# Three places where half-height float32 products of two heads are put side by side in TensorE's queue

## The chip, the cores and the metric

One core of one Trainium2 chip. The metric is the device time of one execution in microseconds (us). The kernel before was run three times: 2778.02, 2770.26 and 2773.04 us, median 2773.04 us.

## The reference, cut to what matters

Two layers, 512 tokens, 1024 channels. Each layer is a feed-forward half step, a mixing step and a second feed-forward half step. The mixing step projects the normed input once and runs three branches on it; the change lies in two of them.

```python
# RWKV-7 branch, 8 heads of 64 channels
w_log = -softplus(-(w0 + tanh(xw) @ decay_b)) - 0.5      # decay: a product over 64 channels
a     = sigmoid(a0 + xa @ iclr_b)                        # in-context rate: a product over 64 channels
...
for t: state = state*w_t - (state @ kk_t) b_t + v_t k_t ; y_t = state @ r_t

# band attention, 8 heads of 64 channels, QK-norm, 512 tokens in chunks of 64
scores = einsum('bnqhd,bnkhd->bnhqk', q, k) * 64**-0.5   # a product over 64 channels
probs  = softmax(scores + bias) ;  out = probs @ v

x = x + W_out(sum_b sigmoid(gate_b) * (y_b @ W_branch_b))
```

The delta-rule scan over time is computed in 8 chunks of 64 steps. A chunk needs the state at its start, a triangular system for the corrections of the chunk, the state at its end, and y of the chunk, which is a sum of two products.

## The kernel before, in words

Heads are worked on two at a time: a tile of 128 partitions holds head u = 0 on partitions 0 to 63 and head u = 1 on 64 to 127 (`H2`; `W2` names the same two halves the other way round). There are four such pairs (`p`) in a layer.

**Big and small products.** The weight products (projections, gates, branch and output matrices, feed-forward) run in float16 with the weight and the input split in a high and a low part, three matmuls for each 128 rows (`mm3`). The RWKV and attention inner products run in float32. A float32 matmul appears in the trace as two instructions, so a row of N products counts 2N.

**The order.** Nothing is issued where it is written. Each call is recorded (`Recorder`, `Plan.note`), and `Plan.run` then simulates the five engines with the costs in `Plan.cost`, always takes the ready operation with the longest tail behind it, and writes out one fixed order for each engine. On TensorE a float16 sum may be put ahead of a small operation when small ones have had more than their share (`RATIO`, `DEBT`). What stands inside one `plan.block()` is one operation for the planner: its matmuls stay together in TensorE's queue, in the order written. Where its simulation sees TensorE idle for more than 0.4 us it puts in filling matmuls (`plan.warm`, on tile `wt`). All instructions are issued from line 538, so profile rows are told apart by tiles and shapes.

**PSUM.** Float16 sums use the buffers `g` (two); `a_ps()` gives one of two buffers for the attention branches (tile `as`), `s_ps()` one of two for RWKV (tile `s`); a ring hands them out in the order of the program, and a buffer waits for the last reader of what it held before. The scan has a bank of its own for y (`yp`) and one for its other products (`xps`).

**The band attention** (`band`). For a pair of heads there are four blocks `b` of 128 queries. `soft(b, u)` takes one buffer, computes the scores of one head (contraction over that head's 64 partitions, 128 queries by `nk = 128 (b + 1)` keys), adds the bias, and does the softmax; `turn` transposes the result in another buffer and copies it out. The units go in the order (b, 0), (b, 1), each `turn` one unit behind its `soft`.

**The RWKV branch** (`rwkv`). For each pair, first the decay: a product over partitions 0 to 63 of `xwa` into a buffer `s`, tanh on ScalarE, plus one on VectorE; then the in-context rate: a product over partitions 64 to 127 into the next buffer `s`, tanh. In the scan each chunk `c` has four blocks on TensorE: x (tiles `ar`, `gx` into `xps`), the corrections (`cx`, `tt`), the state step (`kk`/`kb0` and `ta`/`be`) and y. In y, head u gets first a product over all 128 partitions (`gx` with `vz`), then one over the 64 partitions of the other half (`g1` with `vu`) which adds to it:

```python
for u, h in enumerate(H2):
    o, w = yp[h, c * CH:(c + 1) * CH], W2[u]
    PE.matmul(o, lhsT=gx[:, c, u, CH:2 * CH], rhs=vz[:, c, u, :], start=True, stop=False)
    PE.matmul(o, lhsT=g1[w, c, :], rhs=vu[u][w, c, :], start=False, stop=True)
```

In the profile `vz` is tile `ar`, `g1` is `g`, and `vu` are `kk` and `ta`. The state for chunk c + 1 is written to `ar` by VectorE from `xps` and is what x of the next chunk waits for.

Of the kernel before, what the change touches and what calls it, by code (L numbers as in the profile page):

```python
# [10 lines left out]
AF = mybir.ActivationFunctionType  # L11
# [5 lines left out]
P = 128  # L17
# [8 lines left out]
CH = 64  # L26
# [529 lines left out]
def trunk(tc: tile.TileContext, i: dict, out: bass.AP, dbg: dict | None = None, depth: int = DEPTH):  # L556
    nc = tc.nc
    dbg = dbg or {}
    plan = Plan(tc)
    ctx = ExitStack()  # L560
    V, S, G, PE, D = plan.V, plan.S, plan.G, plan.PE, plan.D
# [42 lines left out]
    def s_ps():  # L604
        return pq.tile([P, T], F32, tag="s", name=nm("s"))

    def a_ps():
        return pa.tile([P, T], F32, tag="a", name=nm("as"))
# [291 lines left out]
    H2 = [slice(0, CH), slice(CH, P)]  # L900
    W2 = [slice(CH, P), slice(0, CH)]
# [69 lines left out]
    def mixing(l, pieces, kst):  # L971
        pv = pvs[l]
        lv = lvs[l]
# [104 lines left out]
        def band():  # L1078
            for p in range(NP):
                q_, k_, vt = att_of[p]  # L1080
                bias = ta_("bias", [P, 2, 2 * P])
                D.dma_start(out=bias, in_=i["bias"][l, p])
                V.memset(bias[0:CH, :, 2 * P - CH:2 * P], -1e30)
                sqs = []
                for t in (k_, q_):
                    sq = ta_("sc", bufs=3)
                    S.activation(sq, t, AF.Square)
                    sqs.append(sq)
                rs = []
                for sq in sqs:  # L1090
                    v = small("n8", 8)
                    V.tensor_scalar(out=v, in0=head_ss(sq, a_ps), scalar1=1.0 / CH, scalar2=1e-6, op0=ALU.mult, op1=ALU.add)
                    rs.append(rpow(v, 8))
                rq = small("rq", 8)
                V.tensor_scalar(out=rq, in0=rs[1], scalar1=CH ** -0.5, scalar2=None, op0=ALU.mult)
                V.scalar_tensor_tensor(out=k_, in0=k_, scalar=lv["aqk"], in1=head_bc(rs[0], a_ps), op0=ALU.mult, op1=ALU.mult)
                pt = []
                for u in range(2):
                    t = ta_("pt", [P, 1280], bufs=2)
                    pt.append([t[:, c0:c0 + T - b * P] for b, c0 in enumerate((0, 512, 896, 1152))])  # L1100

                def soft(b, u):
                    nk = (b + 1) * P
                    h = H2[u]
                    ps = a_ps()
                    PE.matmul(ps[:, :nk], lhsT=q_[h, b * P:(b + 1) * P], rhs=k_[h, 0:nk], start=True, stop=True)
                    sc = ta_("sc", bufs=3)
                    far = max(0, nk - 2 * P)
                    for c0, c1, bb in ((0, far, bias[:, u, 0:1].to_broadcast([P, far])), (far, nk, bias[:, u, 2 * P - (nk - far):2 * P])):
                        if c1 > c0:  # L1110
                            V.scalar_tensor_tensor(out=sc[:, c0:c1], in0=ps[:, c0:c1], scalar=rq[:, 2 * b + u:2 * b + u + 1], in1=bb, op0=ALU.mult, op1=ALU.add)
                    nx = small("nx")
                    V.tensor_reduce(out=nx, in_=sc[:, :nk], op=ALU.max, axis=AX.X, negate=True)
                    den = small("den")
                    S.activation(sc[:, :nk], sc[:, :nk], AF.Exp, bias=nx[:, 0:1], accum_out=den)
                    rd = small("rd")
                    V.reciprocal(rd, den)
                    V.tensor_scalar(out=sc[:, :nk], in0=sc[:, :nk], scalar1=rd[:, 0:1], scalar2=None, op0=ALU.mult)
                    return b, u, sc

                def turn(b, u, sc):
                    ps = a_ps()
                    with plan.block():
                        for kb in range(b + 1):
                            PE.transpose(ps[:, kb * P:(kb + 1) * P], sc[:, kb * P:(kb + 1) * P], ident)
                    for kb in range(b + 1):
                        S.activation(pt[u][kb][:, (b - kb) * P:(b - kb + 1) * P], ps[:, kb * P:(kb + 1) * P], AF.Copy)

                pend = []
                for b in range(4):  # L1130
                    for u in range(2):
                        pend.append(soft(b, u))
                        if len(pend) > 1:
                            turn(*pend.pop(0))
                turn(*pend.pop(0))
                ps = a_ps()
                with plan.block():
                    for kb in range(4):
                        for u in range(2):
                            PE.matmul(ps[H2[u], kb * P:T], lhsT=vt[:, kb, u * CH:(u + 1) * CH], rhs=pt[u][kb], start=(kb == 0), stop=(kb == 3))  # L1140
                y = tm("ya", bufs=5)
                S.activation(y, ps, AF.Copy)
                ya.append(y)
            m2 = small("vx")
            V.tensor_reduce(out=m2, in_=vm, op=ALU.max, axis=AX.X)
            s, d = scale_of_max(all_max(m2), pool=mp, tag="satt")
            for p in range(NP):
                y = tm("ya", [P, 2, T], F16, bufs=5)
                put(y, ya[p], s)
                ya[p] = y  # L1150
            ya.append(d)
# [83 lines left out]
        def rwkv():  # L1235
            for p in range(NP):
# [14 lines left out]
                else:  # L1251
                    D.dma_start(out=vfs[p], in_=v_)

                ps = s_ps()
                PE.matmul(ps, lhsT=glob["lw"][0:CH, cs], rhs=glob["xwa"][0:CH, :], start=True, stop=True)
                tz = tr("w", bufs=3)
                S.activation(tz, ps, AF.Tanh, scale=0.5, bias=lv["w0"][:, p:p + 1])
                V.tensor_scalar(out=tz, in0=tz, scalar1=1.0, scalar2=None, op0=ALU.add)
                ps = s_ps()
                PE.matmul(ps, lhsT=glob["lw"][CH:P, cs], rhs=glob["xwa"][CH:P, :], start=True, stop=True)  # L1260
                ta = tr("ta")
                S.activation(ta, ps, AF.Tanh, scale=0.5, bias=lv["a0"][:, p:p + 1])
                cu = tr("w", bufs=3)
                V.tensor_tensor_scan(out=cu, data0=con[:, C_CM:C_CM + T], data1=tz, initial=0.0, op0=ALU.mult, op1=ALU.add)

# [69 lines left out]
                ps = s_ps()  # L1335
# [41 lines left out]
                for c in range(NCH):  # L1377
                    xp_ = xps[:, 0:3 * CH]
                    with plan.block():
                        for u, w in enumerate(W2):  # L1380
                            PE.matmul(xp_[w, 0:CH], lhsT=gx[:, c, u, 0:CH], rhs=vz[:, c, u, :], start=True, stop=True)
                    x_ = tr("cx", [P, CH], bufs=2)
                    V.tensor_copy(x_, xp_[:, 0:CH])
                    with plan.block():
                        for w in W2:
                            PE.matmul(xp_[w, CH:2 * CH], lhsT=tt[w, c, :], rhs=x_[w, :], start=True, stop=True)
                    S.activation(vu[0][W2[0], c, :], xp_[W2[0], CH:2 * CH], AF.Copy, scale=-1.0)
                    V.tensor_scalar(out=vu[1][W2[1], c, :], in0=xp_[W2[1], CH:2 * CH], scalar1=-1.0, scalar2=None, op0=ALU.mult)
                    if c < NCH - 1:
                        with plan.block():  # L1390
                            for u, w in enumerate(W2):
                                PE.matmul(xp_[w, 2 * CH:3 * CH], lhsT=kb[u][:, c, :], rhs=vu[u][:, c, :], start=True, stop=True)
                        if c:
                            zc = tr("czc", [P, 2, CH], bufs=2)
                            V.tensor_scalar(out=zc, in0=vz[:, c, :, :], scalar1=aw[:, c:c + 1], scalar2=None, op0=ALU.mult)
                        for u, w in enumerate(W2):
                            z = vz[w, c + 1, u, :]
                            if c:
                                V.scalar_tensor_tensor(out=z, in0=xp_[w, 2 * CH:3 * CH], scalar=aw[w, c:c + 1], in1=zc[w, u, :], op0=ALU.mult, op1=ALU.add)
                            elif u:  # L1400
                                V.tensor_scalar(out=z, in0=xp_[w, 2 * CH:3 * CH], scalar1=aw[w, c:c + 1], scalar2=None, op0=ALU.mult)
                            else:
                                S.activation(z, xp_[w, 2 * CH:3 * CH], AF.Copy, scale=aw[w, c:c + 1])
                    with plan.block():
                        for u, h in enumerate(H2):
                            o, w = yp[h, c * CH:(c + 1) * CH], W2[u]
                            PE.matmul(o, lhsT=gx[:, c, u, CH:2 * CH], rhs=vz[:, c, u, :], start=True, stop=False)
                            PE.matmul(o, lhsT=g1[w, c, :], rhs=vu[u][w, c, :], start=False, stop=True)


# [267 lines left out]
```

## Time and profile before

| | |
|---|---|
| median of three runs | 2773.04 us (2770.26 to 2778.02) |
| the profiled execution, its own time | 2773.73 us |
| its span in the trace | 2771.9 us |
| granted TensorE clock, mean | 0.999 |
| TensorE matmuls busy | 2745.1 us, 99% |
| VectorE busy | 1626.2 us, 59% |
| ScalarE busy | 1538.0 us, 55% |
| DMA, mean | 90 GB/s |

The layers' mixing steps with RWKV and attention lie at about 420 to 930 us and 1800 to 2310 us of the span. A matmul's row gives its start as recorded and an end that is modelled, and matmuls overlap; what a piece of work costs TensorE is read from start to start, and not from the durations.

### The profile page before, as it was taken

To read this page: it belongs to the slowest core of one execution; us is meant where nothing else is said; L and a number is where in the kernel's file an instruction comes from. 1 tells how busy PE (TensorE), PEld (TensorE's weight loads), DVE (VectorE), ACT (ScalarE), POOL (GpSimd) and SP (SyncE) were. 2 spreads that over 40 slices of the span, in tenths; PEclk is the share of its full clock that TensorE was granted. 3 is DMA by queue.
4 is the path that set the end of the run, shared out by engine and by line. 5 is a ranking of instruction groups with operands and counts; after the bars stand their busy time and mean duration, and the time that the engine had idled before them with its cause. 6 is when DMAs were issued, how large, how long until landed. Compare 5 with 4: busy or idle time off the path is not lost. (4 is left out here: it accounts for less than half of the span.)

```text
span 2771.9 us, 45458 instructions
## 1 busy us (share of the span) xinstructions
PE 2745.1 (99%) x18153; PEld 1496.6 (54%) x18153; DVE 1626.2 (59%) x4391; ACT 1538.0 (55%) x2543; POOL 111.1 (4%) x285
## 2 busy tenths in 40 slices
PE   9999999999999999999999999999999999999999
PEld 6444486565645456444564444765655454654445
DVE  6344486777766676354463544777776666743543
ACT  6556475565645566565455654655655445655652
POOL 0000000000000000000000000000000000000000
PEclk9999999999999999999999999999999999999999
DMA  4222341111121223222222223311212112232332
GB/s 169 105 93 103 122 140 69 51 61 45 52 83 70 85 98 115 95 104 99 99 107 105 93 106 118 129 52 42 70 35 75 67 54 92 92 114 100 107 106 77
DMA packets 47157, 249.36 MB, mean 90 GB/s; under 512 B 5312, under 2 KB 10688, under 8 KB 23648
## 3 DMA queue, kind: packets, MB, share of 16 engines
q1 hardware_dynamic: 46944, 246.45, 25.2%
q8 instruction: 142, 2.33, 0.3%
q14 instruction: 71, 0.58, 0.1%
HBM read 239.09 MB, written 7.34 MB: 89 GB/s over the span
## 5 line engine op out<-in xcount | busy, mean ns | idle before, releaser
L538 PEld LDWEIGHTS <-wh 128*128 128x128 f16 x10920 | 1047.6, 98 | 1008.0 <-issue 26.8
L538 PE MATMUL g<-hh,wh 128*128 128x512 f16 (+1 forms) x3216 | 987.0, 367 | 0.4 <-DVE k L538 0.4
L538 ACT ACTIVATE wh<-wr,qs 128x1024 f16<-128x1024 f32 (+2 forms) x478 | 484.0, 1050 | 222.5 <-PE g L538 114.3
L538 ACT ACTIVATE junk<-wr 128x2048 uint8<-128x2048 f32 (+2 forms) x239 | 412.9, 1727 | 332.9 <-DMA wr<-ffn_in 144.3
L538 PE MATMUL g<-hl,wh 128*128 128x512 f16 (+1 forms) x1608 | 588.9, 366 | 0.0
L538 DVE SCALAR_TENSOR_TENSOR wh<-wr,qs,wh 128x1024 f16<-128x1024 f32 (+2 forms) x478 | 545.2, 1168 | 43.8 <-ACT wh L538 42.9
L538 PE MATMUL as<-hh,wh 128*128 128x512 f16 (+1 forms) x1536 | 443.3, 361 | 0.0
L538 PE MATMUL as<-hl,wh 128*128 128x512 f16 (+1 forms) x768 | 277.4, 361 | 0.0
L538 PE MATMUL as<-ab,wh 128*128 128x512 f16 (+1 forms) x1224 | 234.7, 350 | 0.0
L538 PE MATMUL g<-ab,wh 128*128 128x512 f16 (+1 forms) x1224 | 234.5, 350 | 0.0
L538 POOL PARTITION_ALL_REDUCE ar<-wm x239 | 97.3, 407 | 2465.5 <-ACT junk L538 2313.6
L538 DVE SCALAR_TENSOR_TENSOR a<-as,md,sg 128x512 f32<-128x512 f32 x44 | 33.0, 750 | 213.3 <-PE as L538 210.0
L538 DVE SCALAR_TENSOR_TENSOR a<-g,md,sg 128x512 f32<-128x512 f32 x44 | 33.0, 750 | 212.9 <-PE g L538 202.7
L538 DVE SCALAR_TENSOR_TENSOR x<-g,md,x 128x512 f32<-128x512 f32 (+1 forms) x62 | 39.0, 628 | 115.8 <-PE g L538 115.8
L538 DVE SCALAR_TENSOR_TENSOR x<-as,md,x 128x512 f32<-128x512 f32 (+1 forms) x62 | 38.9, 628 | 115.8 <-PE as L538 115.8
L538 DVE TENSOR_SCALAR qt<-ar 128x1 int32<-128x1 int32 x253 | 37.6, 150 | 104.0 <-POOL ar L538 101.7
L538 ACT ACTIVATE sq<-x 128x256 f32<-128x256 f32 x96 | 37.0, 407 | 78.9 <-DVE x L538 50.6
L538 ACT ACTIVATE kk<-xps 64x64 f32<-64x64 f32 x64 | 14.0, 219 | 112.6 <-DVE ta L538 93.9
L538 ACT ACTIVATE ti<-s 64x256 f32<-64x256 f32 (+1 forms) x144 | 54.3, 378 | 28.2 <-PE s L538 18.3
L538 DVE SCALAR_TENSOR_TENSOR ab<-a,qs,ab 128x512 f16<-128x512 f32 x88 | 60.7, 746 | 10.3 <-ACT ab L538 10.3
L538 ACT ACTIVATE sg<-as,md 128x512 f32<-128x512 f32 x44 | 30.1, 684 | 56.2 <-PE as L538 56.2
L538 ACT ACTIVATE ab<-a,qs 128x512 f16<-128x512 f32 x88 | 55.9, 709 | 7.3 <-DVE qs L538 7.3
(345 smaller groups left out, 3133.4 us busy)
## 6 DMA issues: line engine op xcount, KB each, us to landing
wr<-ffn_in SPq DMA_DIRECT2D x88, 1024.0 KB, 4.8
wr<-ffn_outa SPq DMA_DIRECT2D x32, 1024.0 KB, 4.9
wr<-w_gate SPq DMA_DIRECT2D x24, 1024.0 KB, 4.9
wr<-w_in SPq DMA_DIRECT2D x22, 1024.0 KB, 4.9
wr<-ffn_outb SPq DMA_DIRECT2D x16, 768.0 KB, 4.3
wr<-w_branch SPq DMA_DIRECT2D x24, 512.0 KB, 3.5
wr<-mem_kv SPq DMA_DIRECT2D x8, 1024.0 KB, 4.9
wr<-w_out SPq DMA_DIRECT2D x8, 1024.0 KB, 4.8
```

Of the source, the lines that this page charges most:

```text
L538: f(*[x.real() if isinstance(x, View) else x for x in a], **{y: x.real() if isinstance(x, View) else x for y, x in k.items()})
```

## The change

Three edits. (1) The scores of both heads of a block `b` are computed by `scores(b)`: two `a_ps()` buffers are taken together and both products stand in one block; `soft` gets its buffer as an argument. (2) The products of the decay and of the in-context rate stand in one block, with two `s_ps()` buffers taken together. (3) In y of the scan the block holds first the two products over 128 partitions, then the two over 64, instead of head after head.

```diff
-                def soft(b, u):
+                def scores(b):
                     nk = (b + 1) * P
-                    h = H2[u]
-                    ps = a_ps()
-                    PE.matmul(ps[:, :nk], lhsT=q_[h, b * P:(b + 1) * P], rhs=k_[h, 0:nk], start=True, stop=True)
+                    pss = [a_ps(), a_ps()]
+                    with plan.block():
+                        for ps, h in zip(pss, H2):
+                            PE.matmul(ps[:, :nk], lhsT=q_[h, b * P:(b + 1) * P], rhs=k_[h, 0:nk], start=True, stop=True)
+                    return pss
+
+                def soft(b, u, ps):
+                    nk = (b + 1) * P
...
                 for b in range(4):
+                    pss = scores(b)
                     for u in range(2):
-                        pend.append(soft(b, u))
+                        pend.append(soft(b, u, pss[u]))
...
-                ps = s_ps()
-                PE.matmul(ps, lhsT=glob["lw"][0:CH, cs], rhs=glob["xwa"][0:CH, :], start=True, stop=True)
+                ps, ps2 = s_ps(), s_ps()
+                with plan.block():
+                    PE.matmul(ps, lhsT=glob["lw"][0:CH, cs], rhs=glob["xwa"][0:CH, :], start=True, stop=True)
+                    PE.matmul(ps2, lhsT=glob["lw"][CH:P, cs], rhs=glob["xwa"][CH:P, :], start=True, stop=True)
...
-                ps = s_ps()
-                PE.matmul(ps, lhsT=glob["lw"][CH:P, cs], rhs=glob["xwa"][CH:P, :], start=True, stop=True)
                 ta = tr("ta")
-                S.activation(ta, ps, AF.Tanh, scale=0.5, bias=lv["a0"][:, p:p + 1])
+                S.activation(ta, ps2, AF.Tanh, scale=0.5, bias=lv["a0"][:, p:p + 1])
...
-                        for u, h in enumerate(H2):
-                            o, w = yp[h, c * CH:(c + 1) * CH], W2[u]
+                        ys = [yp[h, c * CH:(c + 1) * CH] for h in H2]
+                        for u, o in enumerate(ys):
                             PE.matmul(o, lhsT=gx[:, c, u, CH:2 * CH], rhs=vz[:, c, u, :], start=True, stop=False)
+                        for u, (o, w) in enumerate(zip(ys, W2)):
                             PE.matmul(o, lhsT=g1[w, c, :], rhs=vu[u][w, c, :], start=False, stop=True)
```

## Rows read from the trace of the kernel before

**Rows 1.** The page: busy time, share of the span, instructions of each engine
```profile
PE 2745.1 (99%) x18153; PEld 1496.6 (54%) x18153; DVE 1626.2 (59%) x4391; ACT 1538.0 (55%) x2543; POOL 111.1 (4%) x285
```
**Rows 2.** Stretch, us; busy us of PE, PEld, DVE, ACT, POOL; clock, DMA share, GB/s
```profile
420.00:930.00 510.00, 500.72 (x4367) 285.76 (x4365) 357.74 (x1080) 274.68 (x579) 15.99 (x42) 1.00 0.17 60
...
1800.00:2310.00 510.00, 501.23 (x4357) 285.19 (x4357) 361.63 (x1084) 273.92 (x575) 16.34 (x41) 1.00 0.17 57
```
**Rows 3.** The filling matmuls (`wt`) alone, second mixing stretch: PE, PEld, DVE; clock, DMA
```profile
1800.00:2310.00 510.00, 2.66 (x17) 1.65 (x17) 0.00 (x0) 1.00 0.17 57
```
**Rows 4.** Timeline of TensorE, end of a scan: start us, us, engine, operation, count
```profile
2296.69 0.34 PE L538 MATMUL xps<-ar,gx 128*64 128x64 f32 x4
2296.96 0.39 PE L538 MATMUL g<-hh,wh 128*128 128x512 f16 x1
...
2298.36 0.33 PE L538 MATMUL xps<-cx,tt 64*64 64x64 f32 x4
2298.62 0.39 PE L538 MATMUL g<-hh,wh 128*128 128x512 f16 x1
...
2300.02 0.33 PE L538 MATMUL yp<-ar,gx 128*64 128x64 f32 x2
2300.28 0.33 PE L538 MATMUL yp<-kk,g 64*64 64x64 f32 x2
...
2301.05 0.39 PE L538 MATMUL g<-hh,wh 128*128 128x512 f16 x1
```
**Rows 5.** Groups of TensorE by shape: count | busy us, mean ns
```profile
L538 PE MATMUL yp<-ar,gx 128*64 128x64 f32 x256 | 40.3, 239 | 0.0
L538 PE MATMUL s<-ar,be 64*64 64x128 f32 x256 | 15.9, 273 | 0.1
```
**Rows 6.** Timeline, all engines: the state step, y and the next x
```profile
2177.95 0.58 DVE L538 SCALAR_TENSOR_TENSOR ar<-xps,aw,czc 64x64 f32<-64x64 f32 x2
2179.25 0.34 PE L538 MATMUL xps<-ar,gx 128*64 128x64 f32 x4
```
**Rows 7.** Timeline of TensorE in layer 0: decay, rate and scores among float16 matmuls
```profile
421.60 1.13 PE L538 MATMUL s<-xwa,lw 64*128 64x512 f32 x4
422.67 0.39 PE L538 MATMUL g<-hh,wh 128*128 128x512 f16 x1
...
538.94 1.09 PE L538 MATMUL s<-xwa,lw 64*128 64x512 f32 x2
...
540.58 0.49 PE L538 MATMUL as<-ak,aq 64*128 64x128 f32 x4
...
542.26 0.38 PE L538 MATMUL g<-hl,wh 128*128 128x512 f16 x1
542.48 0.38 PE L538 MATMUL g<-hh,wh 128*128 128x512 f16 x1
542.78 1.12 PE L538 MATMUL s<-xwa,lw 64*128 64x512 f32 x2
543.84 0.39 PE L538 MATMUL g<-hh,wh 128*128 128x512 f16 x1
...
544.59 0.70 PE L538 MATMUL as<-ak,aq 64*128 64x256 f32 x2
545.22 0.39 PE L538 MATMUL g<-hh,wh 128*128 128x512 f16 x1
```
**Rows 8.** Groups of TensorE by shape: the largest scores
```profile
L538 PE MATMUL as<-ak,aq 64*128 64x512 f32 x32 | 17.9, 640 | 0.3 <-DVE qt L538 0.3
```
**Rows 9.** Timeline, all engines: what stands between scores and the transposed probabilities
```profile
543.80 0.34 DVE L538 SCALAR_TENSOR_TENSOR sc<-as,rq,bias 128x128 f32<-128x128 f32 x1
...
549.95 0.28 ACT L538 ACTIVATE pt<-as 128x128 f32<-128x128 f32 x1
...
551.14 0.70 PE L538 MATMUL as<-ak,aq 64*128 64x256 f32 x2
```

## The prediction, written before the change was run

> **What bounds the kernel now.** I read the page's busy times first. TensorE is busy for 2745.1 of 2771.9 us, VectorE for 1626.2, ScalarE for 1538.0 [rows 1]. A busy share can hide filling, so the second view is the busy time by stretch. In the two mixing steps TensorE is busy for 500.7 and 501.2 of 510 us, VectorE for 358 and 362, which is 70% [rows 2], and only 2.66 us of the second step (17 instructions) are filling matmuls [rows 3]. So in the stretches that the change touches TensorE idles or fills for some 10 us in each 510, and what leaves TensorE's queue should leave the time, as far as no other engine is late instead. The third view is TensorE's timeline, from start to start, since it shows which products run at once.
>
> **What the timeline says of small float32 products.** The block for x is two products of 128 rows by 64 columns that lie in different column halves; the two take 0.27 us together (2296.69 to 2296.96). The block of corrections is two products of 64 by 64 in different row and column halves; the two take 0.26 us (2298.36 to 2298.62) [rows 4]. In y, where shapes alternate, each of the four products takes as long as such a pair: the first 0.26 us (2300.02 to 2300.28) and all four 1.03 us (2300.02 to 2301.05) [rows 4]. So two neighbours of one shape in different parts of the array share a slot of about 0.26 us; a neighbour of another shape takes its own.
>
> The same holds for 64 rows by 128 columns. One lone decay or rate product of 512 columns takes 1.06 us (542.78 to 543.84), but in two of the eight head pairs both happen to stand together, and the two take 1.07 us (421.60 to 422.67) [rows 7].
>
> **The sum, part by part.**
>
> *y.* 256 instructions of the 128-row form, four in a block, are 64 blocks [rows 5]. A block of four slots becomes one of two: 1.03 minus (0.27 + 0.26) is 0.50 us. 64 x 0.50 = 32.0 us. That the second pair, with rows and columns crossed, shares its slot has no row of y; the nearest is the crossed product `be`, 256 instructions or 128 products of 128 columns in 15.9 us, 0.12 us each [rows 5], under half of the 0.26 us of a lone product of half that width.
>
> *Scores.* The four products of a head have 128, 256, 384 and 512 keys. The two of 128 keys stand together already (540.58, count 4) [rows 7], as in all eight head pairs, so nothing is to be had there. For 256 keys a lone product takes 0.63 us (544.59 to 545.22); for 512 keys I take the 1.06 us of the equal decay shape; for 384 the mean, 0.84 us. Each change of shape also delays the entry: the float16 cadence is 0.22 us (542.26 to 542.48), the step into a 64-row product 0.30 (542.48 to 542.78) [rows 7], so 0.08 more. A removed slot is then worth 0.71, 0.92 and 1.14 us, less 0.01 that a pair takes over a single (1.07 against 1.06): 0.70 + 0.91 + 1.13 = 2.74 us for a head pair. 32 instructions of the largest form are 16 products, so eight head pairs [rows 8]: 21.9 us.
>
> *Decay and rate.* Six of eight pairs are apart; 6 x 1.13 = 6.8 us.
>
> Together 60.7 us. Against the profiled execution's own time, 2773.73 us, that is 2713.0.
>
> **What is late next.** In the scan, y lies between the state step and the next x, and so covers VectorE's writing of the state. In the tightest of the chunks where it does, that write ends at 2178.53 and x starts at 2179.25 [rows 6]: 0.72 us of room, of which 0.50 go. I take 1 us for all 64 blocks; the bounds are 0 and the whole 32.0. The planner's cost of the y block is a sum that doesn't depend on the order inside, so edit (3) by itself moves nothing else.
>
> *Decay and rate* must now take both buffers at once. The decay can't start before the buffer for the rate is free, which in the pair at 538.94 was 3.84 us later (538.94 to 542.78) [rows 7]. It is the largest of six such distances, so the bounds are 0 (float16 sums cover the delay on TensorE) and 6 x 3.84 = 23 us (the RWKV chain sets the end throughout). Both steps being 98% busy with work that may be put there [rows 2, 3], I lie nearer to the cover: 4 us. Tanh, scan and the key norm are behind that wait; on TensorE only what the planner, which knows of the wait, puts after it.
>
> *Scores* take both attention buffers, so scores of block b + 1 can't start before the transposed tile of (b, 0) has been copied out. In the first handover of the second head pair this copy ends at 550.23 (549.95 + 0.28), and the second lone product of the next block stood at 551.14 anyway [rows 9]: there the pair can stand where its later half stood, and the delay is nothing. In the other direction, 24 handovers (three for each of eight head pairs) at up to 6.4 us bare (543.80 to 550.23) [rows 9] are 154 us. I take 3 us, near the cover, since attention has work of other streams beside it at each point.
>
> Edits (1) and (2) also make the planner draw up another order. Which small product falls between which sums is then different, and each changes shape at 0.08 us and more; I put 10 us either way on that as an estimate.
>
> Sum: 2713.0 + 1 + 4 + 3 = 2721, and as the profiled execution lay 0.7 us above the median of the three runs, 2720 us.
>
> **A rule that speaks against the change.** The corrections are two products in different row halves that write one bank, `xps`, and they share their slot of 0.26 us [rows 4]. But they only overwrite; the second pair of y adds to what the first left, in one bank `yp`, from different row halves, and no row shows that. The Trainium skill, page TensorEngine Tiling (Array Packing), section Restrictions and Gotchas, says that different row tiles can't access the same PSUM bank at one time. By that rule the second pair of y would queue; the rows of the corrections go against it, and by them the sum stands as above.
>
> **Rivals.**
>
> *A. The adding pair of y queues* (the mechanism just named). One slot of 0.26 us comes back in each of 64 blocks: 16.6 us, so 2737. For it: no row of adding from two row halves. Against: the overwriting pair. 0.07.
>
> *B. A good part of the gain turns into waits on VectorE.* At 358 busy us in 480 instead of 510, VectorE goes from 70% to 75% [rows 2], and in the dense parts above that. If half of the 60.7 us come back as TensorE waiting for small VectorE steps, the time is 2743. For it: VectorE works in order, and behind a weight split the chain waits. Against: the 0.72 us of room in the tightest handover. 0.12.
>
> *C. Slower: the attention buffers.* If scores can't run ahead and float16 sums run dry because their outputs wait for attention to release its query and value tiles, TensorE stands bare in the 24 handovers. It decides from 60.7 / 24 = 2.5 us each. At half of the 6.4 us, 77 us come, and the time is 2713 + 77 = 2790. Against: the planner knows the buffers and has RWKV, projections and gates to put there. 0.03.
>
> *D. It doesn't do what it says*: neighbours of scores don't overlap with different keys and banks. Then only y pays, 32 us, and the time is 2742 or a little more. Two decay pairs and eight pairs of smallest scores already overlap [rows 7], so 0.02.
>
> *E. No change*: the new order costs about what the pairs bring, 2773. 0.03.
>
> The forecast itself gets 0.73, with a range of its own from 2705 to 2736 (the planner's 10 us either way, and the losses between 0 and 18).
>
> **How the numbers follow.** The range for 8 in 10 goes from 2704 (60.7 us in full, with nothing lost and most of the 10 us on the good side) up to 2743, which takes in A, and B and D at their price; what is left out is C, E, the bad half of B, and a new order that is better or worse than I allow. A measurement of this kernel tells 0.3%, 8.3 us, from no change. Faster by more than that: the forecast, A, B and D, 0.94, less 0.01 for their worst ends, 0.93; within it: E and that, 0.04; slower: C, 0.03.
>
> **What would show it.** In TensorE's timeline after: y as count 4 and count 4, 0.53 us from its start to the next product; scores always as count 4 with about the time of one (0.63, 0.84, 1.06); decay always count 4 with 1.07. The number of float32 instructions is unchanged. Each mixing step is shorter by some 26 us and the stretch between them is not. Step by step wrong would be: y with a third slot (A), longer idle before `xps` in the scan (B), many more than 17 filling matmuls in a mixing step (C), decay later by more than some 4 us in a pair with TensorE idle beside it. The prediction as a whole is wrong if the time is above 2743, or if it is met while the mixing steps aren't what got shorter.

## The result, and the profile after

The changed kernel takes 2745.06 us (median of four runs, 2744.63 to 2745.76) against 2773.94 us for the kernel before (four runs): ratio 0.9896, 95% interval 0.9879 to 0.9913. It is faster by 28.9 us, where 53 were forecast, and 2 us outside the range.

What the change did to TensorE's work is what the sum said. In the timeline of the kernel after, the end of a scan shows y as one slot for the two products over 128 rows and one for the two over 64, 0.53 us from its start to the next product (2276.33 to 2276.86), where it was 1.03 [rows 4]:

```profile
2276.02 0.38 PE L538 MATMUL g<-hh,wh 128*128 128x512 f16 x1
2276.33 0.34 PE L538 MATMUL yp<-ar,gx 128*64 128x64 f32 x4
2276.59 0.27 PE L538 MATMUL yp<-kk,g 64*64 64x64 f32 x1
2276.60 0.27 PE L538 MATMUL yp<-ta,g 64*64 64x64 f32 x1
2276.70 0.22 PE L538 MATMUL yp<-kk,g 64*64 64x64 f32 x1
2276.71 0.22 PE L538 MATMUL yp<-ta,g 64*64 64x64 f32 x1
2276.86 0.39 PE L538 MATMUL g<-hh,wh 128*128 128x512 f16 x1
```

Groups of TensorE by shape in the kernel after (count | busy us, mean ns | idle before): the count is unchanged, and the busy time of the largest scores is halved from 17.9 us [rows 8], that of the first products of y from 40.3 [rows 5]. Decay and rate stand together everywhere.

```profile
L538 PE MATMUL yp<-ar,gx 128*64 128x64 f32 x256 | 19.8, 233 | 0.0
L538 PE MATMUL as<-ak,aq 64*128 64x512 f32 x32 | 9.1, 641 | 0.0
L538 PE MATMUL s<-xwa,lw 64*128 64x512 f32 x32 | 8.9, 634 | 0.0
```

The page's busy line, and the two stretches of [rows 2] (stretch; busy us of PE, PEld, DVE, ACT, POOL; clock, DMA), look as before: TensorE 99% busy.

```profile
PE 2708.5 (99%) x18292; PEld 1479.6 (54%) x18292; DVE 1626.2 (59%) x4391; ACT 1533.3 (56%) x2543; POOL 112.0 (4%) x285
```

```profile
420.00:930.00 510.00, 497.06 (x4512) 284.91 (x4511) 366.44 (x1098) 279.82 (x589) 16.68 (x44) 1.00 0.18 63
1800.00:2310.00 510.00, 496.21 (x4402) 279.71 (x4403) 366.94 (x1096) 279.07 (x587) 17.44 (x43) 0.99 0.18 61
```

But there are 139 instructions more, all of them filling. The same stretches with the filling matmuls alone (PE, PEld, DVE; clock, DMA):

```profile
420.00:930.00 510.00, 15.12 (x97) 9.36 (x97) 0.00 (x0) 1.00 0.18 63
1800.00:2310.00 510.00, 11.19 (x73) 7.03 (x73) 0.00 (x0) 0.99 0.18 61
```

Before, the first stretch had this row, and the second 2.66 us [rows 3]:

```profile
420.00:930.00 510.00, 1.56 (x9) 0.81 (x9) 0.00 (x0) 1.00 0.17 60
```

So 15.12 and 11.19 us of filling stand where 1.56 and 2.66 stood, and TensorE idles for 12.9 and 13.8 us of each 510 instead of 9.3 and 8.8 [rows 2]. One place in layer 0, from the timeline of all engines of the kernel after:

```profile
655.49 0.92 PE L538 MATMUL as<-ak,aq 64*128 64x384 f32 x4
...
656.34 2.10 PE L538 MATMUL xps<-wt 128*128 128x320 f16 x14
...
658.28 0.38 PE L538 MATMUL as<-con,sc 128*128 128x128 f32 x2
...
658.49 1.95 PE L538 MATMUL xps<-wt 128*128 128x320 f16 x13
...
660.72 1.95 PE L538 MATMUL xps<-wt 128*128 128x320 f16 x13
...
664.49 1.13 PE L538 MATMUL as<-ak,aq 64*128 64x512 f32 x4
...
666.34 0.67 ACT L538 ACTIVATE aq<-g,md 128x512 f32<-128x512 f32 x1
...
667.06 0.38 PE L538 MATMUL g<-hh,wh 128*128 128x512 f16 x1
```

Both buffers `g` hold finished sums. The first is copied out at 666.34 into the query tile `aq`, which the last scores (from 664.49 on) have to read first; only after that does the next float16 product come (667.06). In between the planner has little but filling for TensorE: 46 instructions of it and a few small float32 products. So the time was saved on TensorE and in good part handed back as filling and idling. Over the whole program the filling rows (`wt`) grow from 55.5 to 75.3 us and the idle time from 26.8 to 35.5. Each mixing step, taken between the same two points of the program, is shorter by 13 to 14 us (537.8 to 523.9, 543.5 to 530.5), where the prediction had some 26. The experiments ask why.

### The profile page after: what moved, and what is told of

The parts are those of the page before. It is cut to its first block, busy times and chain, and to the rows that moved or that the text cites. A ratio compares the mean times of both kernels' runs of the same rounds, so it can differ in the third digit from the quotient of the medians.

```text
span 2744.0 us, 45718 instructions
## 1 busy us (share of the span) xinstructions
PE 2708.5 (99%) x18292; PEld 1479.6 (54%) x18292; DVE 1626.2 (59%) x4391; ACT 1533.3 (56%) x2543; POOL 112.0 (4%) x285
## 4 chain that ended last, share of the span: by engine, by line
PE 86%; DVE 9%; ACT 2%; issue 2%; DMA 0%; POOL 0%; SPq 0%; ACTq 0%; POOLq 0%; DVEq 0%
PE g L538 45%; PE as L538 33%; PE s L538 4%; PE xps L538 3%; PE yp L538 1%; DVE gx L538 1%; DVE wh L538 1%; DVE w L538 1%; DVE sc L538 1%; DVE rs L538 1%; DVE tt L538 1%; ACT wh L538 0%; DVE be L538 0%; ACT ti L538 0%; ACT pt L538 0%
## 5 line engine op out<-in xcount | busy, mean ns | idle before, releaser
L538 PE MATMUL xps<-wt 128*128 128x320 f16 x476 | 75.3, 306 | 5.3 <-ACT ar L538 1.6
```

What stands on the lines that cost most here:

```text
L538: f(*[x.real() if isinstance(x, View) else x for x in a], **{y: x.real() if isinstance(x, View) else x for y, x in k.items()})
```

## The experiments

All times are medians, with the ratio to the kernel before run on the same chip and its 95% interval; the kernel before had medians of 2772.6 to 2773.9 us in all of these.

**The three edits one by one**

Each takes whole hunks of the change's diff: `only_y` the one in y, `only_scores` those of `scores` and `soft`, `only_decay` the one of `ps2`, `y_decay` the first and the third of these.

```diff
+                        for u, o in enumerate(ys):                            # only_y, y_decay
+                        for u, (o, w) in enumerate(zip(ys, W2)):
...
+                    pss = [a_ps(), a_ps()]                                    # only_scores
...
+                ps, ps2 = s_ps(), s_ps()                                      # only_decay, y_decay
```

> Edit (3) alone, the four products of y regrouped; the order of everything else is that of the kernel before. Theory 1 (TensorE is the limit throughout the mixing steps, the new order of edits 1 and 2 lost the rest): the whole 32 us come, 2742. Theory 2 (in the first part of each mixing step the attention stream, band and then the four memory heads, sets the pace, and what TensorE saves there turns into idling and filling): only the 32 of 64 y blocks that lie behind the end of attention count, 16 us, 2758, and TensorE's idle time in the mixing steps grows by 10 us or more.

Measured: 2740.46 us, ratio 0.9877 (0.9864 to 0.9889): 33.2 us, the whole of the sum's 32.0. Theory 1 holds for this edit, theory 2 falls. Its idle time and filling are those of the kernel before.

> Edit (1) alone, the scores of two heads in one block with both attention buffers. Theory 1: 22 us less, 2752. Theory 2: all scores lie inside the attention stream; it gets shorter by at most a slot for each block of queries, and the rest turns into filling matmuls: 2762 to 2772. Theory 3 (rival C, the two buffers lengthen attention): 2775 or more.

Measured: 2788.47 us, 1.0051 (1.0037 to 1.0065), slower by 14.8. Of the three, only theory 3 had allowed that.

> Edit (2) alone, decay and rate in one block. Theory 1: 6.8 us less, 2767. Theory 2: only the pairs behind the end of attention count, 2 to 3 us less, 2771, within what a new order changes. Theory 3 (the wait for both buffers lengthens the RWKV chain): 2775 to 2785.

Measured: 2781.16 us, 1.0024 (1.0014 to 1.0033), slower by 7.5; again as theory 3.

> Edits (2) and (3) without (1). Theory 1: 39 us less, 2735. Theory 2: 16 to 20 us less, 2754 to 2758, so slower than all three edits together (2745). Theory 3 (taking both attention buffers is what costs): faster than all three together, below 2740.

Measured: 2748.68 us, 0.9905 (0.9892 to 0.9918). None of the three: slower than edit (3) alone by 8, and slower than all three edits by 3.6, so undoing the scores doesn't help here; 3.6 us is less than what another order alone turns out to be worth below.

**Is it what the edits constrain, or that the order is another?** Edits (1) and (2) change what the planner sees, and it draws up another order on all engines; edit (3) doesn't. To see what another order costs by itself, one constant was moved that changes no work and no dependence:

```diff
-    SLACK = 0.04
+    SLACK = 0.041      # y_slack41, b_slack41, all_slack41; 0.039 in y_slack39, b_slack39, all_slack39
```

> Edit (3) alone, and one constant of the planner (the slack added to every hop between engines) at 0.041 instead of 0.040 us: no work and no dependence changes, but the planner draws up another order throughout. Theory N (any new order costs, since the planner's order is sensitive and the one of the kernel before is a good one): 2746 to 2760. Theory C (orders as such are worth a few us; what cost in edits 1 and 2 is that two buffers are taken together): 2737 to 2745, as edit (3) alone (2740).

Measured: 2753.3 us, 0.9924 (0.9909 to 0.9938).

> The same with 0.039 us: a second neutral order. Theory N: 2746 to 2760. Theory C: 2737 to 2745.

Measured: 2748.45 us, 0.9908 (0.9892 to 0.9925). A thousandth of a microsecond in the planner's hops costs 12.8 and 8.0 us. Theory N, as far as two orders can show it.

> Edit (3), and of edit (1) only that both attention buffers are taken together before the scores of a block of queries; the two products stay two operations for the planner and need not be neighbours. Theory C: the constraint costs without the pairs' gain, 2755 to 2775, with more filling matmuls than the 337 of edit (3) alone. Theory N: the same as the two neutral orders.

```diff
                     pss = [a_ps(), a_ps()]
-                    with plan.block():
-                        for ps, h in zip(pss, H2):
-                            PE.matmul(...)
+                    for ps, h in zip(pss, H2):
+                        PE.matmul(...)
```

Measured: 2747.03 us, 0.9902 (0.9888 to 0.9917): no worse than the two neutral orders. Taking both buffers together doesn't cost what theory C said, though it does show more filling (411 matmuls). The two neutral orders differ by 5 us themselves, so a price of a few us can't be seen here.

> All three edits, and the planner counts a pair of scores, or decay and rate, as one slot instead of the sum of two. Theory K (the planner plans each pair at about twice what it takes and so puts filling and waits in the wrong places): 2715 to 2730. If it isn't that: 2740 to 2750, as all three edits.

```diff
-        o.us += self.cost(o, eng, name, outs[0], ins, k)
+        us = self.cost(o, eng, name, outs[0], ins, k)
+        o.us = max(o.us, us) if o.share else o.us + us     # share: the blocks of edits (1) and (2)
```

Measured: 2750.11 us, 0.9916 (0.9901 to 0.9931). Telling the planner that a pair takes one slot doesn't help; theory K falls.

**What is a microsecond of TensorE worth?** These kernels leave the order on VectorE and ScalarE as it is and leave float16 matmuls out of TensorE's queue, the planner's costs unchanged. They do less work than the program needs, and serve only to price TensorE's time:

```diff
                 PE.matmul(ps, lhsT=b, rhs=x, start=False, stop=(k == n - 1))
+                if cut:
+                    plan.cur.calls.pop()       # planned, but not issued
                                                # y_cut_early, b_cut_early: r, k, v of p in (1, 2)
                                                # y_cut_late: gates of b == 2, m < 3
```

> Edit (3) in its order, unchanged on every engine, with 96 float16 matmuls left out of TensorE's queue: the low half of the weight in the r, k and v projections of head pairs 1 and 2 of both layers, which lie in the attention part of each mixing step (96 x 0.216 us = 20.7 us, about what the pairs of scores are worth). Theory P (TensorE still sets the pace once y is regrouped, and edits 1 and 2 lost their gain only by the new order): 2718 to 2723. Theory F (edit (3) has brought the mixing steps down to what the chains through VectorE and ScalarE need, and TensorE's work is no longer what counts there): 2733 or more, with TensorE idling 12 us or more longer.

Measured: 2732.99 us, 0.9851 (0.9834 to 0.9867): 7.5 us of the 20.7, with TensorE idling 10 us longer in the mixing steps. That is theory F's bound for the time, and a little under its 12 us of idling.

> The same with 96 matmuls left out behind attention: the low half of the weight in six of eight gates of the memory branch of both layers (20.7 us). Theory P: 2718 to 2723. Theory F: if the RWKV chain sets the end there, 2733 or more.

Measured: 2729.05 us, 0.9838 (0.9823 to 0.9852): 11.4 us of the 20.7, between the two theories. TensorE's time counts by a third in the attention part and by half behind it, as a mean; the passage on where TensorE is the limit takes the half apart.

**Is attention late?**

```diff
-LIFT = 110
+LIFT = 60       # all_lift60; 140 in all_lift140
```

> All three edits, and RWKV's precedence over attention in the planner at 60 instead of 110 us. Theory A (with all three edits, attention, which must end before the branch sums can be evacuated, is late, and TensorE fills in front of its end): attention ends earlier, 2725 to 2738. Theory N (only the order's luck): anywhere from 2738 to 2755.

Measured: 2790.12 us, 1.0059 (1.0044 to 1.0074). Theory A falls: with attention put forward, its last memory head ends 12 us earlier in layer 0 (745.2 against 757.3 us in the changed kernel), but RWKV's y is finished by VectorE (tile `yr`) 45 us later (959.5 against 914.5).

> The same with 140 us: attention ends later. Theory A: 2752 to 2765. Theory N: 2738 to 2755.

Measured: 2758.63 us, 0.9946 (0.9932 to 0.9961). Slower as well, by 13.6 us. That is inside theory A's range, which the run before has ruled out, but it is also about what a neutral order costs, so this run shows little by itself; only the 45 us of the other one are well clear of that, and lie outside theory N's range too.

**Was y's place special, or was it only first?**

> The kernel before with the planner's slack at 0.041 us, a neutral order without any of the three edits. Theory N (edits 1 and 2 by themselves were slower, 2788 and 2781, because any new order is): 2780 to 2790. Theory C (they were slower by what they constrain): 2768 to 2779.

Measured: 2787.6 us, 1.006 (1.0043 to 1.0077).

> The same with 0.039 us. Theory N: 2778 to 2790. Theory C: 2768 to 2779.

Measured: 2779.86 us, 1.0022 (1.0012 to 1.0033). Theory N, though 0.039 only just. Edits (1) and (2) alone took 2788.47 and 2781.16; the slower of them is within 1 us of the slower neutral order, so another order is enough to explain that they were slower at all.

> The kernel before in its order, without the same 96 float16 matmuls of the r, k and v projections of head pairs 1 and 2 (20.7 us of TensorE), y not regrouped. Theory D (diminishing: before y was regrouped, any 20 us of TensorE counted in full): 2753 to 2756. Theory S (y is a special place: its block stands in the RWKV chain itself, between one chunk's state step and the next chunk's x, while work elsewhere counts only in part even before): 2762 to 2768.

Measured: 2766.25 us, 0.9979 (0.997 to 0.9988): 6.6 us of the 20.7 in the kernel before too. Theory S's time; it isn't that y came first.

> Edit (3) in its order, without the 96 matmuls of the early cut and also without the 16 VectorE steps that make the low halves which these would have read (8 of 1024 and 8 of 512 columns, about 16 us of VectorE). The early cut alone came to 2733. Theory V (behind edit 3 it is VectorE's queue that sets the pace in the attention part): 2722 or less. Otherwise 2730 to 2734.

```diff
             V.scalar_tensor_tensor(out=w[:, 1, a:b], ...)
+            if drop:
+                plan.ops[-1].calls.clear()     # low half planned, but not made
```

Measured: 2730.1 us, 0.9847 (0.9832 to 0.9861), 3 us less than the early cut and within the spread of its runs (2726.49 to 2732.38 against 2731.43 to 2736.1). 16 us of weight splitting on VectorE are not what sets the pace either; theory V is not borne out.

> All three edits under the neutral order of slack 0.041 us, to be set beside edit (3) alone under the same constant (2753.3). If TensorE's time off the RWKV chain counts by a third, as the cuts say (6.6 and 7.5 of 20.7 us), edits 1 and 2 are worth 9 to 10 of their 28.7 us: 2744, with the luck of an order 6 us either way, 2738 to 2750. If they count in full: 2725. If they bring nothing: 2753.

Measured: 2747.78 us, 0.9908 (0.989 to 0.9927): inside the range of "by a third", on the side of less.

> The same with 0.039 us, beside 2748.4: by a third 2739, 2733 to 2745; in full 2720; nothing 2748.

Measured: 2743.0 us, 0.9891 (0.9875 to 0.9907): inside that range again, on the side of less. Three kernels under three values of the constant, in us:

| planner's slack | 0.040 | 0.041 | 0.039 |
|---|---|---|---|
| kernel before | 2773.7 | 2787.6 | 2779.9 |
| edit (3) alone | 2740.5 | 2753.3 | 2748.4 |
| all three edits | 2745.1 | 2747.8 | 2743.0 |

Downwards, y is worth 33, 34 and 31 us in the three orders. Edits (1) and (2) are worth 5.5 and 5.4 us under the two constants where neither row has the order of the kernel before, and cost 4.6 where the row above has it. So an estimate of their own worth is some 5.5 us of 28.7, and of giving up that order 8 to 13. It rests on two pairs of orders.

**Part of what another order costs is the granted clock.** In the profiled execution of `only_scores` TensorE's clock stood at the lower of its two levels (1.2 of 2.4 GHz, 0.50 in the rows) for 45 us. 17 of them are one piece, the stretch in the first line below (busy us of PE, PEld, DVE, ACT, POOL; clock, DMA). In it a float16 matmul took 0.42 us from start to start (2078.67 to 2079.09), instead of 0.22:

```profile
2074.50:2091.60 17.10, 17.10 (x44) 8.38 (x43) 11.06 (x37) 6.66 (x14) 0.00 (x0) 0.50 0.01 1
2078.67 0.63 PE L538 MATMUL g<-hl,wh 128*128 128x512 f16 x1
2079.09 0.63 PE L538 MATMUL g<-hh,wh 128*128 128x512 f16 x1
```

In the kernel before it was 6.8 us, in its two neutral orders 17 each, in edit (3) alone 3.4, in that one's neutral orders 17 and 15, in all three edits 10. Half of such time is lost where TensorE is the limit. By this estimate the clock is up to 19 of the 20 us by which that execution of `only_scores` is longer than the kernel before's, 5 of the 12 and of the 8 us in the two neutral orders of the kernel before, and 7 of 13 and 6 of 7 us in those of edit (3). The six executions of `only_scores` bear it out: at a mean clock of 0.992 they took up to 2793.9 us, at 0.997 2782.1. What brings the clock down stays open: shortly before the fall at 1982.1 us in `b_slack41` TensorE had idled for 2.2 us, but before the one at 2176.6 it hadn't idled since 2170.

With half of the time at the lower clock taken off the profiled executions, edits (1) and (2) bring -1, 5 and 7 us in the three columns, and y 31, 32 and 33. That the edits bring far less than 28.7 us is clear of this spread; the 5.5 isn't.

**Where TensorE is the limit.** The stretches of the first scan and of what follows until the second tell why y is worth all of its time. The kernel before (stretch; busy us of PE, PEld, DVE, ACT, POOL; clock, DMA):

```profile
486.20:528.00 41.80, 41.52 (x340) 23.76 (x339) 25.25 (x94) 22.17 (x52) 1.16 (x3) 1.00 0.19 64
529.00:631.00 102.00, 100.08 (x994) 60.70 (x991) 83.67 (x266) 62.22 (x148) 2.56 (x8) 1.00 0.17 61
```

Edit (3) alone, the same two stretches of its trace:

```profile
484.80:522.60 37.80, 37.52 (x340) 20.83 (x337) 25.26 (x94) 21.77 (x52) 1.15 (x3) 1.00 0.20 71
523.60:625.50 101.90, 99.99 (x992) 60.57 (x989) 83.63 (x266) 62.05 (x147) 2.56 (x8) 1.00 0.18 61
```

Edit (3) with the early cut, and the second stretch of the kernel before with the same cut:

```profile
483.10:520.40 37.30, 37.02 (x338) 20.58 (x335) 25.35 (x95) 21.59 (x52) 1.15 (x3) 1.00 0.21 72
521.40:625.00 103.60, 98.23 (x969) 61.26 (x966) 83.87 (x266) 61.94 (x147) 2.56 (x8) 0.97 0.18 60
527.20:627.60 100.40, 95.39 (x970) 59.14 (x967) 83.64 (x266) 62.03 (x148) 2.56 (x8) 1.00 0.18 62
```

In the scan VectorE is busy 60% of the time, and y's 4.0 us come off the stretch (41.80 to 37.80). In the stretch after it VectorE is busy 82%, working on the next pair's products and on attention together. Leaving 24 instructions (5.2 us) out of TensorE there makes the kernel before's stretch shorter by 1.6 us (102.00 to 100.40), and TensorE idles for 5.0 us instead of 1.9. With y regrouped the stretch didn't get shorter (101.90 to 103.60), but there the clock stood at its lower level for 6.8 us from 595.5, which is up to 3.4 us of it.

Over both layers, TensorE idles for 0.3 of the 259 us in which y blocks follow each other in the kernel before (from a scan's first y to its last, without a pause of 22 us in one), and for 17.8 us in the rest of the mixing steps; with y regrouped the scans come to 228 us, 32 less, and with the early cut the idle time in the rest goes from 18.2 to 28.4 us. These sums are worked out from the starts and gaps of all of TensorE's instructions in those stretches of the traces.

Is it y's chain that makes its time count, or the stretch it lies in? The late cut settles it, since 30 of its 96 matmuls (6.5 us) lie between the first and the last y of a layer's last scan. In layer 0 these two y are here in edit (3) alone, and then with the late cut:

```profile
873.10 0.34 PE L538 MATMUL yp<-ar,gx 128*64 128x64 f32 x4
896.79 0.34 PE L538 MATMUL yp<-ar,gx 128*64 128x64 f32 x4
```

```profile
868.03 0.34 PE L538 MATMUL yp<-ar,gx 128*64 128x64 f32 x4
888.74 0.34 PE L538 MATMUL yp<-ar,gx 128*64 128x64 f32 x4
```

From one to the other it is 23.7 us and then 20.7, and in layer 1 30.7 and 27.5: 6.1 of the 6.5 us come, so in these scans a float16 matmul counts nearly in full too. The 64 matmuls in front of these scans (13.8 us) bring 5.8. It is the stretch that decides, and theory S's reason, y's place in the chain, isn't needed.

## Why the prediction was wrong, point by point

- *y, 32.0 us: right* in size and mechanism. 33, 34 and 31 us came in three orders, and the y blocks of the trace are 0.53 us. Of the 1 us put down for lost room no loss is seen.
- *Rival A, the adding pair queues: wrong.* The two products over 64 rows start 0.01 us apart (2276.59 and 2276.60) and share 0.27 us while adding into one bank from different row halves, each to its own half of the partitions. Here the rule cited from the Trainium skill (TensorEngine Tiling (Array Packing), Restrictions and Gotchas) is not borne out.
- *Scores 21.9 and decay 6.8 us: right as TensorE's time, wrong as time.* TensorE's busy time for the three larger scores falls from 43.5 to 22.0 us and for decay and rate from 15.7 to 8.9. That this leaves the time is the step that failed. The prediction took "TensorE is busy for 500 of 510 us" [rows 2] to mean that what leaves its queue leaves the time. It holds in the scans, where TensorE practically never idles. Elsewhere in the mixing steps a microsecond of TensorE is worth a third (cuts of 20.7 us brought 6.6 and 7.5) to four tenths (5.8 of 13.8 us in front of the last scans). Edits (1) and (2) brought some 5.5 of 28.7 us, a fifth, once set beside neutral orders, and TensorE's filling and idling grew instead. That the rest is chained through VectorE's and ScalarE's steps would fit VectorE's 82% and TensorE's growing idle time, but it is not shown: no run here shortened that chain, and the one that relieved VectorE of 16 us brought 3. Which step decides there stays open.
- *The new order, "10 us either way": right in size, one-sided in these runs.* It was put down as an error around zero and not as a term. The order of the kernel before is better than both neutral ones, by 14 and 6 us without y and by 13 and 8 with it, and by the estimate above up to half of that is time at the lower clock, which the prediction doesn't consider. In the changed kernel's own trace the loss stands as filling and idling, some 20 and 9 us more, and the clock takes only some 2 us more than in the kernel before. A term of about +10 would have stood in the sum.
- *Decay's wait, 4 us, and the buffers of attention, 3 us, and rival C*: taking both attention buffers shows no cost beside the neutral orders (2747.0 against 2753.3 and 2748.4), so that C is wrong as a price. Of decay's wait no run shows the price by itself: edit (2) alone, 2781.2, lies between the neutral orders, and 4 us can't be told from their spread. What rival C said of float16 sums waiting for attention's query tile does happen (655 to 667 us), once TensorE is ahead of attention.
- *Rival B, half of the gain lost to VectorE's waits, 2743*: near in time, by luck. It looked for the loss before `xps` in the scan, where TensorE still idles for only 0.3 us with y regrouped; and that the loss elsewhere is waits on VectorE is not shown.
- *Rival D, the pairs don't overlap, 2742: wrong*, though its time is near. The pairs of scores do overlap: two of 384 keys take 0.85 us (655.49 to 656.34), where the prediction had 0.84 for one.

With what the runs show the sum is 2773.7 - 33 (y) - 5.5 (edits 1 and 2) + 10 (another order) = 2745. Its last two terms are estimates from the table, taken after the result, so that it closes is no test of them.

Edit (3) alone, 2740.5 us, is faster than the changed kernel (2745.1); that this is by its order only is suggested by the two neutral orders, where all three edits are ahead by 5.5, but isn't shown. For this program as it stands edit (3) alone is the faster.

## What to carry to other kernels

Read a busy share by stretch, and ask of each stretch where its idle microseconds are: TensorE was over 99% busy in the one kind, idle 0.3 us in 259, and its time counted in full there; in the other it was 98% busy, and six tenths to two thirds of what it saved were taken back. Products of one shape that lie in different parts of the array belong next to each other, above all in stretches where TensorE never idles. Where a greedy planner writes the order, an edit that it can see is worth its gain less the luck of the present order, so move a constant that means nothing, see what that costs, and see how much of it is the granted clock, before an edit is judged.

## What the runs showed of the hardware that was not expected

Two float32 products that add into one PSUM bank, one from partitions 0 to 63 and one from 64 to 127, each into its own half of the bank's partitions, run at once: 0.27 us for both (2276.59 to 2276.86), as for the overwriting pair of corrections [rows 4].

The mean granted clock goes with the order of the instructions, though the work is the same: the kernel before had 0.997 to 1.000 in all its executions, `b_slack41` 0.995 to 0.997. With edit (1) alone it was 0.992 to 0.997.
